# Attention probabilities of the selected and the window branch in one tile, with one run of keys, in a hybrid sparse-attention layer

## The chip, the cores and the metric

The kernel runs on one core of a Trainium2 chip. The metric is the device time of one execution in microseconds (us), median of several runs. Engines are named as the profile does: PE (TensorE), PEld (its weight loads), DVE (VectorE), ACT (ScalarE), POOL (GpSimd), SP (the queue that issues the DMAs).

## The reference, cut to what matters

One decoder layer on 512 rows of 1024 features. One projection of the normed input feeds two groups of eight heads of 64. The first group (NSA) attends in three branches with the same queries; each has its own keys and values, and its output is scaled by a gate:

```python
o_cmp, p_cmp = compressed_branch(qn, kc_cmp, vc_cmp)      # 31 compressed blocks
o_sel = selected_branch(qn, ks_r, heads(vs, G), sel_idx)  # top 16 of 8 blocks: all causal keys
o_win = window_branch(qn, kw_r, heads(vw, G))             # window 512 on 512 rows: all causal keys
o_nsa = g[..., 0:1] * o_cmp + g[..., 1:2] * o_sel + g[..., 2:3] * o_win
```

With these sizes the selected and the window branch are both plain causal attention over up to 512 keys. The second group (DSA) attends to the 128 keys with the highest indexer score:

```python
score = einsum('bths,bth->bts', relu(qi @ ki), wi)         # the indexer, 4 heads
_, idx = lax.top_k(where(causal, score, NEG), 128)
```

Both outputs are multiplied by their own SiLU gates, go through one output projection and are added to the input.

## The kernel before, in words

Every float32 operand of a product is split in two parts (hi and lo, of type fp32r), and a product is the sum of two or three products of parts, so nearly everything on PE comes in pairs or threes.

**Stages.** (1) `x` arrives; the projection of the indexer's columns (`I`) and the row norms. (2) Projection chunks `C` (raw compressed keys, line 400), `B` (keys and values of selected and window, line 390), with the indexer between them (lines 591, 612, 690) and its top-128 on DVE (lines 701 and 702), which gives masks. (3) Chunks `Q1`, `Q2`, `D` (queries), the compression network (`hid`, line 777), and from the end of `Q2` on the attention, woven with `D`, four gate chunks `Z` and the output projection (line 1220).

**Attention.** The work is cut in units: `n` or `d` (the group), query tile `i` of 128 rows, key head `g`, and for `n` a branch `b` (1 selected, 2 window, 0 compressed). The tiles' names carry them: `P_n302` is n, i=3, g=0, window. A unit goes through four blocks of 32 queries times 4 heads, which make 128 rows:

- Scores: `softmax_steps` multiplies a block's queries with the keys in `kn` (line 1011, two products hi and lo). Block `b` of tile `i` sees `128 i + 32 b + 32` keys. For i > 0 selected and compressed keys lie side by side and share a product, and the window's keys have their own; for i = 0 a copy of the window's first tile (two DMAs, `K_WIN0`) puts all three side by side, and each block multiplies all 288 columns.
- `softmax_of`: mask, scale and row minimum on DVE (line 983), a memset of the tile's ragged end (line 987), the exponential with its row sum on ACT (line 988), the reciprocal on DVE, and normalisation times the gate on POOL (line 1001). The probabilities `P` go to one of three rotating buffers, one per unit.
- `transposed`: for each key tile of 128, four PE transposes (line 1030) of the four blocks fill one PSUM bank; ACT copies it to `pth` (line 1031), DVE puts the rest in `ptl` (line 1032). Both have three buffers (`TBUFS`).
- `times_values`: two products of 512 columns (line 1041) with the values of that key tile, hi and lo side by side as 128 columns, add to the PSUM bank `o`.

For query tile i a selected and a window unit have i + 1 key tiles each. The last is the rows' own tile, in which block 0 sees 32 keys, block 1 64, block 2 96, block 3 128.

```python
us.v = [pair(vsw[:, j, g]) for j in range(i + 1)]
uw.v = [pair(vsw[:, j, 2 + g]) for j in range(i + 1)]
uw.S = lambda: softmax_steps(q, lambda b: [(k[:, :, 0:keys(b)], [win_(b)])])
```

**The order.** `attention` interleaves scores of later units with transposes and products of the present one, and `weave` fills other work in. Then `set_order` plans again: from a table of costs and due times it writes out a fixed order for every engine and for the DMA queue (`ROUNDS` passes; `URGENT`, `SOON`: when an engine waits for a more urgent instruction; `HURRY`: nanoseconds by which a named output is due earlier, empty here). An engine then executes its list strictly in order.

**Other lines that are spoken of.** `values_of` (lines 856 and 857) evacuates values, `kstack` and `key_parts` (lines 579 to 582, 591, 593) write transposed keys, `rope` (lines 532 to 538) rotates, `chunk_C` turns raw keys into compression inputs `FS` (lines 754 to 766), line 548 transposes the row norms.

Of the kernel before, what the change touches and what calls it, by code (L numbers as in the profile page):

```python
# [9 lines left out]
F32 = mybir.dt.float32  # L10
# [52 lines left out]
ARENA = 3689  # L63
# [3 lines left out]
RTB = 4  # L67

COST = 1 / 2400
TBUFS, AHEAD, LAG = 3, 2, 2  # L70
# [16 lines left out]
URGENT, SOON = 3000, 400  # L87
# [16 lines left out]
HURRY = {}  # L104
# [204 lines left out]
def tile_hybrid_layer(ctx, tc, xT, x, ng, win, gains, peT, w1, b1, w2, wout, cst, out):  # L309
# [128 lines left out]
    tri = carve([S + 384], BF16)  # L438
# [69 lines left out]
    trib = carve([S], BF16)  # L508
    nc.gpsimd.memset(trib, 0.0)
    nc.gpsimd.tensor_copy(trib[:, S - 32:], cs[:, C_TRIB:C_TRIB + 32])  # L510
# [6 lines left out]
    def tables(j, name):  # L517
        gn = gns[:, j, None, :]
        tab = work.tile([128, 2, NT, HD], F32, tag="tab", name="tab", bufs=3)
# [7 lines left out]

    def rope(dst, src_ps, nh, ct, st, p=128, add=None, tag="rt", wide=4):

        t2 = work.tile([128, wide, HD], F32, tag=tag + "2", name=tag + "2", bufs=RTB if tag == "rt" else 1)[:p, :nh, :]  # L530
# [53 lines left out]
    def kstack(dst, R, h0, nh):  # L584

        p = ps("T", "kT_ps")
        for t in range(NT):
            c = t * 128
            if nh == 1:

                nc.tensor.transpose(p[:, c:c + 128], R[:, t, h0:h0 + 2, :], ident)
            else:
                nc.tensor.transpose(p[:, c:c + 128], R[:, t, h0:h0 + nh, :], ident)
        if nh == 1:
            hi, lo = dst[0]
            nc.scalar.copy(hi, p)
            nc.vector.tensor_tensor(lo, p, hi.bitcast(F32), op=ALU.subtract)
            return
        for g in range(nh):
            key_parts(dst[g], p[g * HD:(g + 1) * HD, :], g)  # L600
# [252 lines left out]
    def values_of(p, t, dst):  # L853

        src_ = p.rearrange("p (c d) -> p c d", d=HD)
        nc.scalar.activation(dst[:, :, 0, :], src_, AF.Copy, scale=rstd[:, t:t + 1])
        nc.vector.scalar_tensor_tensor(dst[:, :, 1, :], src_, rstd[:, t:t + 1], dst[:, :, 0, :].bitcast(F32),
                                       op0=ALU.mult, op1=ALU.subtract)
# [17 lines left out]
    def b1_first():  # L876
        load_w1(0)
        ST["kb_raw"] = [work.tile([128, NT, 2, HD], F32, tag="m2", name=f"kb_raw{b}", bufs=2) for b in range(2)]
# [10 lines left out]

    def kb_stack():  # L890
        for b in range(2):
            kstack([two(k, slice(0, S) if b else slice(K_SEL, None)) for k in kn], ST["kb_raw"][b], 0, 2)
            if b:
                for k in kn:
                    nc.sync.dma_start(k[:, :, K_WIN0:K_CMP].bitcast(F32), k[:, :, 0:128].bitcast(F32))
            yield 0.4
# [72 lines left out]
    def softmax_of(u, b, src_, mask):  # L969

        n = src_.shape[-1]
        if b == 0:
            if u.b == 0 and u.kind == "n":
                u.P = pcs[:, turn_c[0] % (AHEAD + 1)]
                turn_c[0] += 1
            else:
                tag, bufs = ("P0", 4) if u.name[:2] == "n0" else ("P", AHEAD + 1)
                w = 128 * u.i + 128
                u.P = work.tile([128, 4, w], F32, tag=tag, name="P_" + u.name, bufs=bufs)
            u.m, u.l = mls[:, turn[0] % 8, 0], mls[:, turn[0] % 8, 1]  # L980
            turn[0] += 1
        P, m, l = u.P[:, b, :n], u.m, u.l
        nc.vector.tensor_tensor_reduce(P, src_, mask, u.r[:, b:b + 1], 3e38, op0=ALU.add, op1=ALU.min,  # L983
                                       accum_out=m[:, b:b + 1])
        if b == 0 and u.P.shape[-1] > 32:

            nc.vector.memset(u.P[:, 0:3, u.P.shape[-1] - 96:], 0.0)
        nc.scalar.activation(P, P, AF.Exp, bias=m[:, b:b + 1], scale=-1.0, accum_out=l[:, b:b + 1])  # L988
        if b == 3:
# [7 lines left out]
            else:  # L997

                for bb in range(4):
                    Pb = u.P[:, bb, :128 * u.i + 32 * bb + 32]  # L1000
# [15 lines left out]
    def transposed(u, j, parts):  # L1016
# [11 lines left out]
        else:  # L1028
            for h in range(4):
                nc.tensor.transpose(p[:, h * 128:(h + 1) * 128], u.P[:, h, j * 128:(j + 1) * 128], ident)  # L1030
            nc.scalar.copy(ph, p)  # L1031
            nc.vector.tensor_tensor(pl, p, ph.bitcast(F32), op=ALU.subtract)  # L1032
        parts.append((u, j, ph, pl))

    def times_values(u, j, *parts):
        if u.first and j == 0:
            u.o[0] = ps("O", "o" + u.name)
        o = u.o[0]
        end = u.last and j == len(u.v) - 1
        for x, pp in enumerate(parts):  # L1040
            nc.tensor.matmul(o, u.v[j], pp, start=(u.first and j == 0 and x == 0), stop=(end and x == 1))  # L1041
        if end:
            if u.dst is None:
                u.dst = work.tile([128, 2, 128], F32, tag="od", name="od_" + u.name, bufs=2)
# [5 lines left out]
    def pv_steps(u, parts):  # L1050

        for j in range(len(u.v) if u else LAG):
            if u:
                transposed(u, j, parts)
# [21 lines left out]
    def units_of(kind, i, g, done):  # L1076
        n = 128 * (i + 1)
        q, o = [None], [None]
        res = []
        order = (1, 2, 0) if kind == "n" else (0,)  # L1080
        for b in order:
# [3 lines left out]
            u.q, u.o, u.done = q, o, done  # L1085
# [12 lines left out]
        causal = lambda b: trib[:, S - keys(b):]  # L1098
        if kind == "d":
            u.v = [pair(vd[:, j, g]) for j in range(i + 1)]  # L1100
            if g == 0 and i:

                mm = work.tile([128, 4, n], BF16, tag="mm", name=f"mm{i}", bufs=2)
# [7 lines left out]
        us, uw, uc = res  # L1111
        us.v = [pair(vsw[:, j, g]) for j in range(i + 1)]
        uw.v = [pair(vsw[:, j, 2 + g]) for j in range(i + 1)]
        uc.v = [pair(vcs[:, g])]
        k = kn[g]
        sel = lambda b, c: (us, slice(c, c + keys(b)), causal(b))
        win_ = lambda b: (uw, slice(0, keys(b)), causal(b))
        cmp = lambda b, c: (uc, slice(c, c + 32), cmask[:, 30 - 8 * i - 2 * b:62 - 8 * i - 2 * b])

        if i == 0:  # L1120
            us.S = lambda: softmax_steps(q, lambda b: [
                (k[:, :, K_WIN0:K_SEL + 128], [sel(b, 160), win_(b), cmp(b, 128)])])
        else:
            uw.S = lambda: softmax_steps(q, lambda b: [(k[:, :, 0:keys(b)], [win_(b)])])
            us.S = lambda: softmax_steps(q, lambda b: [
                (k[:, :, K_CMP:K_SEL + keys(b)], [sel(b, 32), cmp(b, 0)])] if keys(b) + 32 <= 512 else [
                (k[:, :, K_SEL:], [sel(b, 0)]), (k[:, :, K_CMP:K_SEL], [cmp(b, 0)])])
# [33 lines left out]
    def attention(units):  # L1161
# [8 lines left out]
        for k in range(-AHEAD, len(units) + 1):  # L1170
# [5 lines left out]
            yield from interleave(pv, itertools.chain(*s), 2 * len(u.v) if u else 1, 5)  # L1176
# [17 lines left out]
    def mix(half, i, g):  # L1194

        o = on[i, g] if half == 0 else od[f"{i}{g}"]
        m = b8.tile([128, 2, 2, 128], F32R, tag=f"mx{half}{g}", name="mx", bufs=2)
# [84 lines left out]
    weave(att, "n000", [  # L1282
# [17 lines left out]
    for i in (2, 1, 0):  # L1300
        weave(att, f"n{i}10", [out_half(i + 1, 0)], RA, X3)
# [98 lines left out]
```

## Time and profile before

| | |
|---|---|
| median of 3 runs | 312.7 us (312.56 to 312.94) |
| the profiled execution's own time | 312.76 us |
| its span, first to last instruction | 311.0 us, granted TensorE clock 1.000 |
| PE, PEld busy | 306.0, 258.9 us |
| DVE, ACT, POOL busy | 263.0, 241.0, 234.6 us |
| DMA | 32.16 MB, 103 GB/s |

The profiled execution is 0.06 us above the median and 1.8 us longer than its span. A matmul's duration in a row is that of one instruction from entry to its modelled end, and matmuls overlap; what one costs PE is the distance from its start to the next one's start, which the timeline shows.

### The profile page before, as it was taken

Reading aid. Unit: us, or ns where it says so; the run is one execution under the profiler, and the core shown is the slowest. Engines: PE = TensorE matmul, PEld = TensorE weight load, DVE = VectorE, ACT = ScalarE, POOL = GpSimd, SP = SyncE. Lnnn points to the kernel's source line nnn. Section 1 sums busy time; section 2 is a strip of 40 time slices with the busy share of each in tenths; the row PEclk is TensorE's granted clock in tenths of the full one; section 3 lists DMA queues with packets and bytes.
Section 4 is the critical chain, followed back from the end, with each engine's and each line's share of the span. In section 5 each row is a group of like instructions: output and inputs, shape, how many; then the busy total and the mean of one; then the engine's idle time right before and its main releaser. Section 6 shows DMA issues by size and latency. Waiting matters only on the chain.

```text
span 311.0 us, 6033 instructions
## 1 busy us (share of the span) xinstructions
PE 306.0 (98%) x1681; PEld 258.9 (83%) x1681; DVE 263.0 (85%) x797; ACT 241.0 (78%) x794; POOL 234.6 (75%) x416
## 2 busy tenths in 40 slices
PE   8999999999999999999999999999999999999995
PEld 4997788999888878888888888888888888888885
DVE  4998635699999999999999999999999999886501
ACT  6964656879997999898999989874379997985500
POOL 2099897997997599894789978995779895767500
PEclk9999999999999999999999999999999999999999
DMA  7994353552421033400031042233445252012011
GB/s 283 414 366 119 100 179 107 163 178 70 119 54 34 2 86 94 144 2 3 16 89 36 5 136 74 72 106 87 134 109 163 70 166 81 4 45 90 8 62 67
DMA packets 21249, 32.16 MB, mean 103 GB/s; under 512 B 5664, under 2 KB 8480, under 8 KB 21216
## 3 DMA queue, kind: packets, MB, share of 16 engines
q1 hardware_dynamic: 21216, 31.78, 32.6%
q8 instruction: 13, 0.21, 0.3%
q14 instruction: 20, 0.16, 0.2%
HBM read 29.04 MB, written 2.47 MB: 101 GB/s over the span
## 4 chain that ended last, share of the span: by engine, by line
PE 88%; DVE 7%; issue 1%; ACT 1%; DMA 1%; DVEq 0%; ACTq 0%
PE out L1220 15%; PE z L400 14%; PE Q L390 11%; PE on L1041 7%; PE D L390 7%; PE B L390 6%; PE s_n L1011 6%; PE T_n L1030 6%; PE od L1041 3%; PE T_d L1030 3%; PE s_d L1011 3%; PE hid L777 2%; DVE xsq L471 1%; PE idx L690 1%; PE qT_ps L612 1%
## 5 line engine op out<-in xcount | busy, mean ns | idle before, releaser
L988 ACT ACTIVATE P_n<-P_n,arena 128x416 f32<-128x416 f32 (+9 forms) x64 | 33.5, 524 | 5.7 <-DVE arena L983 3.5
L983 DVE CUSTOM_DVE_ANT_0 P_n<-s_n,arena 128x416 f32<-128x416 f32 (+9 forms) x64 | 30.7, 492 | 2.0 <-PE s_n L1011 1.2
L1001 POOL TENSOR_SCALAR P_n<-P_n,arena 128x416 f32<-128x416 f32 (+7 forms) x64 | 30.4, 493 | 1.5
L1011 PE MATMUL s_n<-kn,arena_r 128*128 128x288 f32 (+12 forms) x116 | 28.6, 326 | 0.0
L1032 DVE TENSOR_TENSOR ptl<-T_n,pth 128x512 fp32r<-128x512 f32 x40 | 27.0, 677 | 0.5 <-ACT pth L1031 0.4
L701 DVE MAX8 m<-scores 128x8 f32<-128x512 f32 (+2 forms) x48 | 26.6, 554 | 0.7
L400 PE MATMUL z<-hThi,whi_Z 128*128 128x512 f32 x64 | 26.4, 413 | 0.0
L702 DVE MATCH_REPLACE8 scores<-m,scores 128x512 f32<-128x512 f32 (+2 forms) x48 | 26.0, 542 | 0.1
L1030 PE MATMUL T_n<-arena,P_n 128*128 128x128 f32 x160 | 26.0, 272 | 0.0
L400 PE MATMUL z<-hTlo,whi_Z 128*128 128x512 f32 x64 | 25.5, 398 | 0.0
L400 PE MATMUL z<-hThi,wlo_Z 128*128 128x512 f32 x64 | 25.3, 398 | 0.0
L1031 ACT CAST pth<-T_n 128x512 fp32r<-128x512 f32 x40 | 23.2, 584 | 1.5 <-PE T_n L1030 1.2
L1011 PEld LDWEIGHTS s_n<-kn,arena_r 128*128 128x128 f32 x116 | 20.9, 188 | 4.0
L1030 PEld LDWEIGHTS T_n<-arena,P_n 128*128 128x128 f32 x160 | 20.2, 140 | 4.9 <-POOL P_n L1001 0.2
L1220 PE MATMUL out<-whi_wo,mx 128*128 128x512 f32 (+1 forms) x72 | 24.2, 384 | 0.0
L1220 PE MATMUL out<-wohi,mx 128*128 128x512 f32 (+1 forms) x72 | 23.9, 375 | 0.0
L357 POOL TENSOR_TENSOR wlo_Z<-raw_Z,whi_Z 128x512 fp32r<-128x512 f32 x16 | 20.5, 1294 | 3.5 <-ACT whi_Z L356 3.5
L390 PE MATMUL Q<-wlo_Q,hThi 128*128 128x256 f32 (+1 forms) x64 | 22.0, 343 | 0.0
L390 PE MATMUL Q<-whi_Q,hTlo 128*128 128x256 f32 (+1 forms) x64 | 21.8, 341 | 0.0
L390 PE MATMUL Q<-whi_Q,hThi 128*128 128x256 f32 (+1 forms) x64 | 21.8, 341 | 0.0
L357 POOL TENSOR_TENSOR w1l<-raw_w,w1h 128x512 fp32r<-128x512 f32 x16 | 20.6, 1300 | 0.0
L988 ACT ACTIVATE P_d<-P_d,arena 128x416 f32<-128x416 f32 (+15 forms) x32 | 16.7, 521 | 5.0 <-DVE arena L983 4.9
(264 smaller groups left out, 1101.5 us busy)
## 6 DMA issues: line engine op xcount, KB each, us to landing
raw_w<-in_w_dram SPq DMA_DIRECT2D x16, 256.0 KB, 3.6
raw_Z<-in_win_dram SPq DMA_DIRECT2D x16, 256.0 KB, 2.7
wor<-in_wout_dram SPq DMA_DIRECT2D x16, 256.0 KB, 2.8
raw_Q<-in_win_dram SPq DMA_DIRECT2D x12, 256.0 KB, 2.9
raw_D<-in_win_dram SPq DMA_DIRECT2D x8, 256.0 KB, 2.9
xres<-in_x_dram SPq DMA_DIRECT2D x8, 256.0 KB, 2.9
out_dram<-xres SPq DMA_DIRECT2D x7, 256.0 KB, 2.0
xw<-in_xT_dram SPq DMA_DIRECT2D x2, 860.0 KB, 7.9
```

What stands on the lines that cost most here:

```text
L357: engine.tensor_tensor(lo, raw, hi.bitcast(F32), op=ALU.subtract)
L390: nc.tensor.matmul(out_ps, a[:, k, tsl], b, start=(k == 0 and b is hi and a is hT["hi"]), stop=(k == KB - 1 and a is hT["lo"]))
L400: nc.tensor.matmul(out_ps, b[:, csl], a[:, k, :], start=(k == 0 and b is hi and a is hT["hi"]), stop=(k == KB - 1 and b is lo))
L701: nc.vector.max(m8, sc)
L983: nc.vector.tensor_tensor_reduce(P, src_, mask, u.r[:, b:b + 1], 3e38, op0=ALU.add, op1=ALU.min, accum_out=m[:, b:b + 1])
L988: nc.scalar.activation(P, P, AF.Exp, bias=m[:, b:b + 1], scale=-1.0, accum_out=l[:, b:b + 1])
L1001: nc.gpsimd.tensor_scalar(Pb, Pb, l[:, bb:bb + 1], 1.0 if u.gate is not None else 0.5, op0=ALU.mult, op1=ALU.mult)
L1011: nc.tensor.matmul(p, q[0][:, b], k[:, x], start=(x == 0), stop=(x == 1))
L1030: nc.tensor.transpose(p[:, h * 128:(h + 1) * 128], u.P[:, h, j * 128:(j + 1) * 128], ident)
L1032: nc.vector.tensor_tensor(pl, p, ph.bitcast(F32), op=ALU.subtract)
L1041: nc.tensor.matmul(o, u.v[j], pp, start=(u.first and j == 0 and x == 0), stop=(end and x == 1))
L1220: nc.tensor.matmul(p, a, b[:, csl], start=(k == 0 and b is hi and a is mx[0]), stop=(k == 7 and a is mx[1]))
```

## The change

For i and g the probabilities of the selected and the window branch lie in one tile of `256 i + 256` columns. Blocks 0 and 1 keep only the first 64 keys of the own tile, and these 64 of selected and 64 of window lie side by side, so that one transpose and one product serve both branches; the values for it (`vm`: selected's first 64 rows above, window's first 64 below) are gathered by two DMAs of 256 KB. Blocks 2 and 3 still have an own tile for each branch. To make the window's part start with the own tile, its keys are stored from the last tile to the first with the halves of a tile exchanged, and its values with exchanged halves. Window keys, compressed keys and selected keys then are one run in `kn`, so that for i < 2 one score product per block serves all three while they fit 512 columns; the two DMAs to `K_WIN0` go. The window branch scores 64 or 128 keys of the own tile instead of 32, 64, 96, 128. The own tile's products have 256 columns.

Besides: `TBUFS` 3 to 2, `URGENT` 3000 to 2000, `SOON` 400 to 300, `HURRY` 4000 for the indexer's score banks, the units of i = 0 run compressed first, and `P`, `od`, tables and rope temporaries have a name each in place of rotating buffers.

```diff
-TBUFS, AHEAD, LAG = 3, 2, 2
+TBUFS, AHEAD, LAG = 2, 2, 2
-URGENT, SOON = 3000, 400
+URGENT, SOON = 2000, 300
-HURRY = {}
+HURRY = {'idx': 4000}
...
-    trib = carve([S], BF16)
+    trib = carve([2 * S + 32], BF16)
...
 def values_of(p, t, dst, parts=((slice(0, 128), slice(0, 128)),)):
+        for a, b in parts:
+            nc.scalar.activation(dst[b, :, 0, :], src_[a], AF.Copy, scale=rstd[a, t:t + 1])
...
-        values_of(p[:, 256:], t, vsw[:, t])
+        values_of(p[:, 256:384], t, vsw[:, t, 0:2])
+        a, b = slice(0, 64), slice(64, 128)
+        values_of(p[:, 384:], t, vsw[:, t, 2:4], ((a, b), (b, a)))
...
+        for x in range(2):
+            h = slice(64 * x, 64 * x + 64)
+            nc.sync.dma_start(ST["vm"][h].bitcast(F32), v[h, :, 2 * x:2 * x + 2])
...
-        if b == 0 and u.P.shape[-1] > 32:
+        if b == 0 and u.kind == "d":
             nc.vector.memset(u.P[:, 0:3, u.P.shape[-1] - 96:], 0.0)
+        if b == 0 and u.kind == "n" and u.b == 1:
+            nc.vector.memset(u.P[:, 0:3:2, 128 * u.i + 96:128 * u.i + 128], 0.0)
...
+            for b, c in blocks:
+                nc.tensor.transpose(p[:, b * 128:(b + 1) * 128], u.P[:, b, c:c + 128], ident)
+            cols = slice(128 * blocks[0][0], 512)
+            nc.scalar.copy(ph[:, cols], p[:, cols])
+            nc.vector.tensor_tensor(pl[:, cols], p[:, cols], ph[:, cols].bitcast(F32), op=ALU.subtract)
...
+        half = lambda b: 64 if b < 2 else 128
+        us.c0 = lambda b: 128 - half(b)
+        uw.c0 = lambda b: 128 * i + 128
+        uw.keys = lambda b: 128 * i + half(b)
+        us.items = [tile_of(us, 128 * j, v(j, 0)) for j in range(i)]
+        uw.items = [([(b, uw.c0(b) + half(b) + 128 * (i - 1 - j)) for b in range(4)], [(whole, v(j, 1))]) for j in range(i)]
+        lo_, hi_ = slice(0, 256), slice(256, 512)
+        uw.items.append(([(b, 128 * i + (64 if b < 2 else 0)) for b in range(4)], [(lo_, ST["vm"][:, i, g]), (hi_, v(i, 0))]))
+        uw.items.append(([(b, 128 * i + 128) for b in (2, 3)], [(hi_, v(i, 1))]))
...
+        if i < 2:
+            res[0].S = lambda: softmax_steps(q, lambda b: [
+                (k[:, :, S - nw(b):K_SEL + ns(b)], [sel(b, nw(b) + 32), win_(b), cmp(b, nw(b))])]
+                if nw(b) + 32 + ns(b) <= 512 else rest_(b) + [(k[:, :, at_w(b)], [win_(b)])])
```

How the order of the instructions moves, at the two places that the prediction speaks of.

PE, the own tile of query tile 1, g = 0 (`T_n`: a bank of transposes, `on`: the output bank, `pth` and `ptl`: the transposed probabilities, `arena_r`: values). Before, the transposes of the own tile of the selected and then of the window branch, and further on their products:

```order
L1030 MATMUL T_n_2267<-arena,P_n_2055 128x128 x4
...
L1030 MATMUL T_n_2340<-arena,P_n_2190 128x128 x4
...
L1041 MATMUL on_2322<-pth,arena_r 128x512
...
L1041 MATMUL on_2322<-ptl,arena_r 128x512
```

Now, the shared tile, the rest of the window's own tile, and their products:

```order
L1054 MATMUL T_n_2321<-arena,P_n_2055 128x128 x4
...
L1054 MATMUL T_n_2364<-arena,P_n_2055 128x128 x2
...
L1068 MATMUL on_2358<-pth,vm 128x256
L1068 MATMUL on_2358<-ptl,vm 128x256
L1068 MATMUL on_2358<-pth,arena_r 128x256
L1068 MATMUL on_2358<-ptl,arena_r 128x256
```

Eight transposes have become six, and four products of 512 columns (a `pth` and a `ptl` for either branch) have become six of 256: the four shown, and a pair with `arena_r` for the window's blocks 2 and 3.

PE, from the transposes of the row norms (`rrow_ps`) to the indexer's key transposes (`kT_ps`) and query transposes (`qT_ps`), with chunk `C` around them. Before:

```order
L548 MATMUL rrow_ps<-arena 128x128 x4
...
L400 MATMUL C_451<-hThi,wlo_C_323 128x512
L591 MATMUL kT_ps<-arena,ridx 128x128 x2
L400 MATMUL C_451<-hThi,whi_C_330 128x512
...
L612 MATMUL qT_ps<-arena,ridx 128x128 x2
```

Now:

```order
L555 MATMUL rrow_ps<-arena 128x128 x4
...
L621 MATMUL qT_ps<-arena,ridx 128x128
...
L401 MATMUL C_453<-hTlo,whi_C_324 128x512
L598 MATMUL kT_ps<-arena,ridx 128x128 x4
L401 MATMUL C_453<-hThi,wlo_C_325 128x512
...
L699 MATMUL idx_570<-kix,arena_r 128x512
```

Between `rrow_ps` and the first key transpose stand 28 products of 512 columns before (3 of `C`, 13 of `B`, 12 of `C`) and 21 now (3, 10 and 8), with two query transposes among them. All four key transposes now stand together, and the indexer's first score product (`idx`) follows five products of `C` later; before, it came behind all of chunk `B`.

## Rows read from the trace of the kernel before

**Rows 1.** The page, busy time of each engine, and the clock by 40 slices

```profile
PE 306.0 (98%) x1681; PEld 258.9 (83%) x1681; DVE 263.0 (85%) x797; ACT 241.0 (78%) x794; POOL 234.6 (75%) x416
PEclk9999999999999999999999999999999999999999
```

**Rows 2.** Stretches: us, busy PE, PEld, DVE, ACT, POOL (instructions), clock, DMA share, GB/s

```profile
20.00:45.00 25.00, 24.64 (x113) 19.63 (x113) 17.56 (x61) 11.73 (x39) 23.66 (x26) 1.00 0.53 166
45.00:70.00 25.00, 25.00 (x153) 22.04 (x152) 17.86 (x43) 19.36 (x66) 22.30 (x36) 1.00 0.50 150
95.00:156.00 61.00, 61.00 (x332) 51.07 (x331) 58.45 (x211) 56.84 (x239) 48.45 (x106) 1.00 0.17 47
200.00:260.00 60.00, 60.00 (x325) 50.91 (x325) 57.46 (x175) 46.38 (x128) 48.99 (x65) 1.00 0.38 111
```

**Rows 3.** All waits of PE: us in total, times, longest us

```profile
PE I L443 <- DVE arena L445: 1.4, 1, 1.4
PE kT_ps L591 <- DVE FS L766: 0.4, 1, 0.4
```

**Rows 4.** Timeline of PE in the attention: start us, us, instruction

```profile
200.74 0.46 PE L1011 MATMUL s_n<-kn,arena_r 128*128 128x320 f32 x2
201.04 0.60 PE L1030 MATMUL T_d<-arena,P_d 128*128 128x128 f32 x4
201.39 0.48 PE L400 MATMUL z<-hThi,whi_Z 128*128 128x512 f32 x1
201.71 0.39 PE L400 MATMUL z<-hTlo,whi_Z 128*128 128x512 f32 x1
...
202.18 0.39 PE L1041 MATMUL od<-pth,arena_r 128*128 128x512 f32 x1
202.41 0.40 PE L1041 MATMUL od<-ptl,arena_r 128*128 128x512 f32 x1
202.64 0.39 PE L400 MATMUL z<-hThi,whi_Z 128*128 128x512 f32 x1
```

**Rows 5.** Timeline of PE at the end, products of 256 columns, nine from start to start

```profile
306.01 0.40 PE L1220 MATMUL out<-wohi,mx 128*128 128x256 f32 x2
...
307.07 0.40 PE L1220 MATMUL out<-wohi,mx 128*128 128x256 f32 x2
```

**Rows 6.** Groups of PE and PEld by line: count, busy us, mean ns

```profile
L1030 PE MATMUL T_n<-arena,P_n 128*128 128x128 f32 x160 | 26.0, 272 | 0.0
L1041 PEld LDWEIGHTS on<-ptl,arena_r 128*128 128x128 f32 x48 | 9.1, 189 | 1.0
```

**Rows 7.** Timeline of PE and DVE before the indexer

```profile
25.09 0.15 DVE L434 COPY arena<-vx_ps 128x4 f32<-128x4 f32 x1
...
25.29 0.65 PE L548 MATMUL rrow_ps<-arena 128*128 128x128 f32 x4
...
27.45 0.42 DVE L532 TENSOR_TENSOR rt<-I,arena 128x256 f32<-128x256 f32 x1 [0.30 <-ACT rest L631]
...
31.98 1.26 DVE L766 TENSOR_TENSOR FS<-ff,FS 128x496 fp32r<-128x496 f32 x2
32.05 0.39 PE L400 MATMUL C<-hThi,wlo_C 128*128 128x512 f32 x1
...
32.80 0.41 PE L591 MATMUL kT_ps<-arena,ridx 128*128 128x128 f32 x2 [0.36 <-DVE FS L766]
```

**Rows 8.** Groups of DVE and ACT by line: count, busy us, mean ns

```profile
L987 DVE MEMSET P_n<- 128x288 f32 x16 | 4.8, 298 | 0.2
L1032 DVE TENSOR_TENSOR ptl<-T_n,pth 128x512 fp32r<-128x512 f32 x40 | 27.0, 677 | 0.5 <-ACT pth L1031 0.4
L857 DVE SCALAR_TENSOR_TENSOR arena_r<-Q,arena,arena_r 128x128 fp32r<-128x128 f32 x4 | 1.4, 351 | 0.4 <-ACT arena_r L856 0.3
L1031 ACT CAST pth<-T_n 128x512 fp32r<-128x512 f32 x40 | 23.2, 584 | 1.5 <-PE T_n L1030 1.2
```

**Rows 9.** The top-128 by its line: ns min/median/max, first and last start us

```profile
L701 DVE MAX8 m<-scores x48: 414/552/696, 62.8 to 229.9; 128x8 f32<-128x512 f32 x16, 128x8 f32<-128x384 f32 x16, 128x8 f32<-128x256 f32 x16
```

More of the change, by code (lines that the diff above doesn't have):

```diff
@@ L877, in b1_first @@
         load_w1(0)
-        ST["kb_raw"] = [work.tile([128, NT, 2, HD], F32, tag="m2", name=f"kb_raw{b}", bufs=2) for b in range(2)]
+        ST["kb_raw"] = [work.tile([128, NT, 2, HD], F32, tag=f"kb_raw{b}", name=f"kb_raw{b}", bufs=1) for b in range(2)]
         ST["ss_kb"] = sums("kb")
@@ L1014, in softmax_steps, with transposed @@
                 yield 2 * COST * max(n, 256)
-    def transposed(u, j, parts):
+    def transposed(u, item, parts):
         p = ps("T", "T_" + u.name)
@@ L1028, in transposed, with times_values @@
         else:
[L1029 to L1036, printed above, removed]
+            blocks = item[0]
+            for b, c in blocks:
[3 more added lines that the diff above has]
+            nc.vector.tensor_tensor(pl[:, cols], p[:, cols], ph[:, cols].bitcast(F32), op=ALU.subtract)
+        parts.append((u, item, ph, pl))
+    def times_values(u, item, *parts):
+        first = u.o[0] is None
+        if first:
             u.o[0] = ps("O", "o" + u.name)
         o = u.o[0]
-        end = u.last and j == len(u.v) - 1
-        for x, pp in enumerate(parts):
-            nc.tensor.matmul(o, u.v[j], pp, start=(u.first and j == 0 and x == 0), stop=(end and x == 1))
+        end = u.last and item is u.items[-1]
+        for cols, v in item[1]:
+            for x, pp in enumerate(parts):
+                nc.tensor.matmul(o[:, cols], v, pp[:, cols], start=(first and x == 0), stop=(end and x == 1))
         if end:
             if u.dst is None:
-                u.dst = work.tile([128, 2, 128], F32, tag="od", name="od_" + u.name, bufs=2)
+                u.dst = work.tile([128, 2, 128], F32, tag="od_" + u.name, name="od_" + u.name, bufs=1)
                 od[u.name[1:3]] = u.dst
@@ L1050, in pv_steps @@
     def pv_steps(u, parts):
-        for j in range(len(u.v) if u else LAG):
+        for item in (u.items if u else [None] * LAG):
             if u:
-                transposed(u, j, parts)
+                transposed(u, item, parts)
                 yield 0.43
@@ L1084, in units_of @@
             u.name = f"{kind}{i}{g}{b}"
-            u.q, u.o, u.done = q, o, done
+            u.q, u.o, u.done, u.pair = q, o, done, pair_
+            u.c0 = lambda b: 0
+            u.keys = lambda b: 128 * i + 32 * b + 32
             u.dst = on[i, g] if kind == "n" else None
@@ L1097, in units_of @@
         keys = lambda b: 128 * i + 32 * b + 32
-        causal = lambda b: trib[:, S - keys(b):]
+        causal = lambda b: trib[:, S + 64 - keys(b):S + 64]
+        whole = slice(0, 512)
+        tile_of = lambda u, c, v: ([(b, u.c0(b) + c) for b in range(4)], [(whole, v)])
         if kind == "d":
-            u.v = [pair(vd[:, j, g]) for j in range(i + 1)]
+            u.items = [tile_of(u, 128 * j, pair(vd[:, j, g])) for j in range(i + 1)]
             if g == 0 and i:
-                mm = work.tile([128, 4, n], BF16, tag="mm", name=f"mm{i}", bufs=2)
+                mm = work.tile([128, 4, n], BF16, tag=f"mm{i}", name=f"mm{i}", bufs=1)
                 v = mbias[i].rearrange("(b r) n -> r b n", b=4)
@@ L1110, in units_of @@
             return res
[L1111 to L1114, printed above, removed]
+        us, uw, uc = (res[order.index(b)] for b in (1, 2, 0))
+        half = lambda b: 64 if b < 2 else 128
+        us.c0 = lambda b: 128 - half(b)
+        uw.c0 = lambda b: 128 * i + 128
+        uw.keys = lambda b: 128 * i + half(b)
+        v = lambda j, b: pair(vsw[:, j, 2 * b + g])
+        us.items = [tile_of(us, 128 * j, v(j, 0)) for j in range(i)]
@@ L1117, in units_of @@
-        win_ = lambda b: (uw, slice(0, keys(b)), causal(b))
+        nw, ns = uw.keys, us.keys
+        own = lambda b: trib[:, 0:nw(b)] if b % 2 else trib[:, S + 32:S + 32 + nw(b)]
+        sel = lambda b, c: (us, slice(c, c + ns(b)), causal(b))
+        win_ = lambda b: (uw, slice(0, nw(b)), own(b))
         cmp = lambda b, c: (uc, slice(c, c + 32), cmask[:, 30 - 8 * i - 2 * b:62 - 8 * i - 2 * b])
-        if i == 0:
-            us.S = lambda: softmax_steps(q, lambda b: [
-                (k[:, :, K_WIN0:K_SEL + 128], [sel(b, 160), win_(b), cmp(b, 128)])])
-        else:
[L1124 to L1127, printed above, removed]
+        at_w = lambda b: slice(S - nw(b), S)
@@ L1175, in attention @@
             pv = pv_steps(u, parts) if k >= 0 else ()
-            yield from interleave(pv, itertools.chain(*s), 2 * len(u.v) if u else 1, 5)
+            yield from interleave(pv, itertools.chain(*s), 2 * len(u.items) if u else 1, 5)
     wo = {}
```

83 lines of the change are left out of this document (48 added, 35 removed).

## The prediction

> **What bounds the kernel.** I read first the page's busy times: PE 98% of the span, DVE 85%, ACT 78%, POOL 75%, the TensorE clock full in every slice [rows 1]. A busy PE need not be a PE at its limit, so I read next what PE waited for: in 311 us the profile names two waits, 1.4 us at the very start and 0.36 us before the indexer's key transposes [rows 3]. Then the timeline, for what an instruction costs PE from its start to the next one's: the two products of 512 columns at 202.18 and 202.41 take 0.23 us each, the one after them starts at 202.64 [rows 4]. So PE runs back to back from about 20 us to the end, and every microsecond of PE work that goes shortens the run, if the other engines keep up. Last, the stretches: from 95 to 156 us DVE is busy for 58.45 of 61 us and ACT for 56.84, from 200 to 260 us DVE for 57.46 of 60 [rows 2]. DVE is nearly a second bound there. Its free time lies early: 7.4 us from 20 to 45 and 7.1 us from 45 to 70 [rows 2], while the top-128 starts only at 62.8 us and ends at 230 [rows 9].
>
> **What PE sheds.** The counts are those of the code; there are 8 pairs of i and g.
>
> Transposes: per pair 4 (2i + 2) before and 4 (2i + 1) + 2 now, 2 less, 16 in all. A group of four followed by a product of 512 starts at 201.04, and the product after that at 201.71: 0.67 us less the product's 0.23 leaves 0.44, or 0.11 us a transpose [rows 4]. That is 1.76 us. (The 272 ns of the group's row [rows 6] is entry to end, with overlap.)
>
> Products with values: per pair four of 512 become six of 256. 32 x 0.23 = 7.36 us go. Nine products of 256 columns with changing weights take 306.01 to 307.07, 0.118 us each [rows 5], so 48 x 0.118 = 5.66 us come. Gain 1.7 us.
>
> Scores: 12 products fewer; the columns of all score products fall by 512, because the merged runs of i = 0 and 1 save more than the window's 64 extra columns per pair and pass cost. Two products of 320 take 0.30 us [rows 4], 0.47 ns a column, so 0.24 us; four products become so narrow (128 columns) that they cost a transpose's 0.11 rather than 0.06 us, which gives back 0.2. I take 0.1 us gain.
>
> Sum: 1.76 + 1.7 + 0.1 = **3.6 us** of PE work.
>
> The Trainium skill has a rule against this: its page "TensorE: Matmul & The Clock Gate", section "Back-to-back issue gap", says that in a stream with weight loads a product of 512 columns costs about 131 ns and one of 128 about 81, so that width costs little and count much. On a line through these two (an estimate) transposes give 1.3 us, scores 0.8, and the products with values lose 0.5, in all 1.6 us instead of 3.6. The trace does not agree: 0.23 us at 512 columns and 0.118 at 256, nearly in proportion.
>
> **What the other engines get.** DVE: of the 16 memsets (298 ns) eight go and eight shrink to 64 columns, at least 2.4 us gone [rows 8]; eight of the 40 subtractions into `ptl` halve, at half of 677 ns some 2.7 us; the evacuation of chunk `B`'s values adds 12 operations of 128 columns or fewer for 4 of 256, at 351 ns [rows 8] at most 4.2 us more, but these lie before 70 us, where DVE has room [rows 2]. The window's 64 extra columns per pair add 512 columns to each of mask, exponential and normalisation, at `ptl`'s 677 / 512 = 1.3 ns a column 0.7 us each. ACT: eight copies into `pth` halve, 8 x 584 / 2 = 2.3 us less [rows 8], against up to 4.2 us more before 70 us. So in the attention DVE sheds 2.4 + 2.7 - 0.7 = 4.4 us and ACT 2.3 - 0.7 = 1.6, while PE sheds 3.6, and the earlier indexer lets the top-128 use DVE's free 14.5 us before 70 us. I count no wait for them there, and none saved, since before shows none on PE [rows 3]. The cover is PE's own work; should it be gone, it is DVE at 58 of 61 us that shows next. POOL gets one more small cast and some memset before 20 us and 0.7 us of normalisation; it stands at 75% [rows 1]. On SP's queue the two `kn` copies go, and two `vm` transfers wait for the last values of `B`; behind them stand the last weight loads of the compression network and of `Q2`, which are not used before the next two chunks; cost nothing.
>
> **What the early indexer costs.** Before, the key transposes waited 0.36 us, because their bank came free with the first `FS` of line 766, which starts at 31.98 [rows 7]. Now PE comes to them after seven products fewer, 7 x 0.23 = 1.6 us, less 0.2 for the query transposes in between: 1.4 us earlier. The `FS` chain stands at the same place in DVE's list. If it ends when it did, PE waits 1.4 us longer. It may end sooner: the ropes no longer alternate with ACT's copies, which cost DVE 0.30 us twice, once at 27.45 [rows 7]. On the other side, the row norms' last copy (25.09 [rows 7]) now stands behind three more small rope operations, some 0.15 to 0.2 us each by its own row, and PE's `rrow_ps` behind it, at most 0.5 us. So the loss lies between nothing, or 0.4 us gained should the old wait vanish, and 1.4 + 0.5 = 1.9 us, with 0.4 on top for each of two query evacuations that may slip in ahead on DVE: 2.7. I take **0.6 us**, nearer to the lower end, since both gaps of 0.30 and the old wait's 0.36 come off the 1.9 and the chain has less around it.
>
> **Sum.** 312.76 (profiled) - 3.6 + 0.6 = 309.8; the median before is 0.06 lower, so **309.7 us**. Bounds: all of the early loss absent and the old wait gone, 312.7 - 3.6 - 0.4 = 308.7, with the row-to-row spread of the durations (0.1 us on each of the three terms) and some of DVE's lighter load showing, 308.1; the early loss at its worst, 312.7 - 3.6 + 2.7 = 311.8.
>
> **The rivals.**
>
> *Two buffers instead of three.* `pth` and `ptl` now have two. In the planned order the transposes of an item stand before the last product of the item two before it in 60 of 66 cases (with three buffers: 11 of 65), so ACT's copy must wait for PE, PE's next product for ACT's 584 ns and DVE's 677 [rows 8], and on ACT the exponentials queue behind the copy. That closes a loop of 0.58 + 0.68 + 0.23 = 1.5 us plus three hand-overs. For it: ACT is 93% busy from 95 to 156 us [rows 2], so a held copy hurts. Against it: an item's share of the attention's 190 us is 190 / 68 = 2.8 us. It decides once PE loses 3.0 us by it: 8 waits like the one of 0.36 [rows 3] make no change, 10 make it slower, 12 give 312.7 - 3.0 + 4.3 = 314.0 us. Chance 0.08.
>
> *Products do not shrink with their width.* If a product of 256 must sit out its own weight load, it costs 0.189 us [rows 6] and not 0.118: 48 x 0.189 = 9.1 us for 7.36, a loss of 1.7 where I have a gain, and 312.7 - 1.76 - 0.1 + 1.7 + 0.6 = 313.1 us. Against it: the nine of [rows 5] have such loads too. Chance 0.02. A milder form is a fixed share in each product: a line through a transpose's 0.11 us at 128 columns and 0.23 at 512 [rows 4] gives 0.15 at 256, so the products with values gain 7.36 - 7.2 = 0.16 instead of 1.7, the scores 12 x 0.07 + 512 x 0.31 ns = 1.0, and the run takes 312.7 - 1.76 - 0.16 - 1.0 + 0.6 = 310.4 us. Chance 0.05. The section of the Trainium skill's page "TensorE: Matmul & The Clock Gate" named above has this form with a flatter line; by its 1.6 us the run would take 311.7. [rows 5] speak against both.
>
> *The change doesn't do what it says.* PE's saved time is idle because DVE, at 58.45 of 61 us [rows 2], paces the attention after all: its work there falls by about 2.4 + 2.7 - 0.7, but the top-128, if not really earlier, stays. Then what goes of DVE's idle share (2.5 of 61) is all that can be gained, near 0.4 us with the early loss on top: 312.7 us. Chance 0.06.
>
> *DVE's relief shows.* Small unnamed stretches between products also close: under 308.1 us. Chance 0.04.
>
> **How the numbers follow.** The forecast with its early loss has 0.75 and spans 308.1 to 311.8, and the fixed share's 0.05 lies inside. What is outside is 0.08 + 0.02 + 0.06 + 0.04 = 0.20. A measurement here tells 0.2%, 0.6 us, from no change: faster is under 312.1. Faster: 0.75 + 0.05 + 0.04 + a part of the "not what it says" case, 0.02 = 0.86. Same: 0.04 of that case and 0.02 of the weight loads, 0.06. Slower: 0.08.
>
> **What the profile after would show.** Right: 144 transposes of `T_n` at line 1054 where line 1030 had 160, 48 products of 256 columns 0.118 us apart, PE still without named waits after 40 us, the first top-128 row well before 62.8 us, DVE's busy share in the attention below 95%, one or two waits of PE between 25 and 35 us of 0.3 to 1.5 us together. Wrong: PE waits at the products with `pth` (the two buffers), products of 256 columns 0.19 us apart, or PE waits at line 1054 for POOL or DVE.

## The result and the profile after

| | before | after |
|---|---|---|
| median | 312.63 us (312.27 to 312.94, 4 runs) | 308.24 us (308.08 to 308.48, 4 runs) |
| profiled execution, span | 312.76, 311.0 us | 308.21, 306.4 us |

The ratio is 0.986 (95% interval 0.9847 to 0.9872): 4.4 us faster, 1.5 us below the forecast of 309.7 us and just above the lower end of its range, 308.1.

The page and the stretches of the changed kernel, beside [rows 1] and [rows 2]. First the busy times:

```profile
PE 301.3 (98%) x1669; PEld 256.4 (84%) x1669; DVE 261.0 (85%) x797; ACT 240.7 (79%) x802; POOL 235.4 (77%) x418
```

Then the stretches (us, busy PE, PEld, DVE, ACT, POOL with instructions, clock, DMA share, GB/s):

```profile
20.00:45.00 25.00, 24.93 (x117) 19.93 (x116) 22.26 (x70) 14.68 (x40) 23.35 (x25) 1.00 0.53 171
45.00:70.00 25.00, 25.00 (x158) 22.68 (x157) 23.50 (x63) 20.51 (x79) 24.69 (x38) 1.00 0.57 156
...
95.00:156.00 61.00, 61.00 (x337) 51.44 (x335) 57.27 (x207) 58.18 (x246) 50.53 (x106) 1.00 0.21 56
...
200.00:260.00 60.00, 60.00 (x323) 50.72 (x321) 52.30 (x157) 45.52 (x125) 45.51 (x61) 1.00 0.37 112
```

PE is still the bound, 98% of a span that is 4.6 us shorter. DVE works earlier: 22.26 and 23.50 us in the first two stretches where [rows 2] have 17.56 and 17.86, and 52.30 instead of 57.46 late. The top-128 by its line (ns min/median/max, first and last start) begins 18 us earlier than in [rows 9]:

```profile
L710 DVE MAX8 m<-scores x48: 412/549/697, 44.6 to 219.2; 128x8 f32<-128x512 f32 x16, 128x8 f32<-128x384 f32 x16, 128x8 f32<-128x256 f32 x16
```

The own tile of one pair in the timeline of PE (start us, us, instruction), four of its six products:

```profile
181.05 0.29 PE L1068 MATMUL on<-pth,vm 128*128 128x256 f32 x1
181.17 0.28 PE L1068 MATMUL on<-ptl,vm 128*128 128x256 f32 x1
181.29 0.28 PE L1068 MATMUL on<-pth,arena_r 128*128 128x256 f32 x1
181.41 0.28 PE L1068 MATMUL on<-ptl,arena_r 128*128 128x256 f32 x1
181.52 0.40 PE L401 MATMUL z<-hThi,whi_Z 128*128 128x512 f32 x1
```

From 181.05 to 181.52 four products take 0.47 us, 0.118 each, as forecast. The groups by line (count, busy us, mean ns, idle before and what ended it), beside [rows 6] and [rows 8]:

```profile
L1054 PE MATMUL T_n<-arena,P_n 128*128 128x128 f32 x144 | 24.1, 273 | 0.0
L1057 DVE TENSOR_TENSOR ptl<-T_n,pth 128x512 fp32r<-128x512 f32 x32 | 21.8, 680 | 3.0 <-ACT pth L1056 2.6 <-POOL arena L1016 0.2
...
L1056 ACT CAST pth<-T_n 128x512 fp32r<-128x512 f32 x32 | 18.7, 583 | 2.5 <-PE od L1068 1.6 <-PE on L1068 0.6
...
L1057 DVE TENSOR_TENSOR ptl<-T_n,pth 128x256 fp32r<-128x256 f32 x8 | 3.3, 416 | 0.6 <-ACT pth L1056 0.4
...
L1056 ACT CAST pth<-T_n 128x256 fp32r<-128x256 f32 x8 | 2.9, 365 | 0.3 <-PE T_n L1054 0.2
```

The two buffers do show, but on ACT and DVE: the copy into `pth` now waits for a product that still reads its buffer (1.6 + 0.6 us for the banks `T_n`), which it did not in [rows 8]. No wait of PE for either has a row.

The early part, beside [rows 7]; first DVE, then PE:

```profile
25.30 0.15 DVE L435 COPY arena<-vx_ps 128x4 f32<-128x4 f32 x1
25.38 0.74 DVE L539 TENSOR_TENSOR rt<-I,arena 128x256 f32<-128x256 f32 x2
...
27.36 1.83 DVE L764 TENSOR_TENSOR kt<-C,arena 64x256 f32<-64x256 f32 x4
...
30.55 0.67 DVE L776 TENSOR_TENSOR FS<-ff,FS 128x496 fp32r<-128x496 f32 x1
```

```profile
25.51 0.65 PE L555 MATMUL rrow_ps<-arena 128*128 128x128 f32 x4
...
31.10 0.60 PE L598 MATMUL kT_ps<-arena,ridx 128*128 128x128 f32 x4
```

`FS` starts 1.43 us earlier than before (31.98), the ropes stand in pairs and both gaps of 0.30 us are gone, and the key transposes at 31.10 have no wait behind their row. They start before the first `FS` has ended (30.55 + 0.67 = 31.22), so they no longer wait for it. All waits of PE now:

```profile
PE I L444 <- DVE arena L446: 1.2, 1, 1.2
PE Q L391 <- DVE kn L587: 0.6, 1, 0.6
```

The 0.36 us at `kT_ps` of [rows 3] are gone, and a new wait has come. Its place, PE and then DVE:

```profile
91.04 0.28 PE L787 MATMUL hid<-w1h,FS 128*128 128x256 f32 x1
91.95 0.47 PE L391 MATMUL Q<-whi_Q,hThi 128*128 128x512 f32 x1 [0.62 <-DVE kn L587]
```

```profile
88.38 0.54 DVE L711 MATCH_REPLACE8 scores<-m,scores 128x384 f32<-128x384 f32 x1
89.67 0.29 DVE L539 TENSOR_TENSOR rt<-Q,tab 128x128 f32<-128x128 f32 x1 [0.74 <-DMA dr_q<-nz]
...
91.45 0.35 DVE L868 SCALAR_TENSOR_TENSOR arena_r<-Q,arena,arena_r 128x128 fp32r<-128x128 f32 x1
```

From 91.04 to 91.95 are 0.91 us where a product of 256 columns leaves 0.12: 0.8 us lost. DVE stood still for 0.74 us before 89.67, for a DMA, and the last of its rows that reads `Q`, at 91.45, ends at 91.80, just ahead of PE's start. The row names `kn`, which follows at 91.71 on DVE. In the program the product waits for the semaphore value that the evacuation at 91.45 sets, and it writes the PSUM bank that this evacuation empties.

One more difference is in no named row: from the start of a product of 512 columns to the start of the next one are 232.4 ns on average before (626 such pairs after 20 us, those over 300 ns left out) and 230.2 ns after (606), in chunk `B` 233.2 and 227.4. What these 2.2 ns are is the subject of the last experiments.

### The profile page after: what moved, and what is told of

Same layout as the page of the kernel before. It is cut to its first block, busy times and chain, and to the rows that moved or that the text cites. A ratio compares the mean times of both kernels' runs of the same rounds, so it can differ in the third digit from the quotient of the medians.

```text
span 306.4 us, 5994 instructions
## 1 busy us (share of the span) xinstructions
PE 301.3 (98%) x1669; PEld 256.4 (84%) x1669; DVE 261.0 (85%) x797; ACT 240.7 (79%) x802; POOL 235.4 (77%) x418
## 4 chain that ended last, share of the span: by engine, by line
PE 86%; DVE 4%; ACT 4%; POOL 3%; DMA 2%; issue 1%; DVEq 0%; POOLq 0%
PE out L1268 15%; PE z L401 14%; PE Q L391 8%; PE D L391 7%; PE B L391 7%; PE on L1068 7%; PE s_n L1033 6%; PE T_n L1054 5%; PE od L1068 3%; PE T_d L1054 3%; PE s_d L1033 3%; PE C L401 2%; PE hid L787 2%; ACT hThi L467 2%; POOL wlo_Q L358 2%; PE idx L699 1%
## 5 line engine op out<-in xcount | busy, mean ns | idle before, releaser
L1010 ACT ACTIVATE P_n<-P_n,arena 128x416 f32<-128x416 f32 (+15 forms) x64 | 33.7, 528 | 4.7 <-DVE arena L1003 4.1
L1003 DVE CUSTOM_DVE_ANT_0 P_n<-s_n,arena 128x416 f32<-128x416 f32 (+15 forms) x64 | 31.0, 499 | 1.0 <-PE s_n L1033 0.4
L1023 POOL TENSOR_SCALAR P_n<-P_n,arena 128x416 f32<-128x416 f32 (+15 forms) x64 | 30.8, 501 | 1.2
L1057 DVE TENSOR_TENSOR ptl<-T_n,pth 128x512 fp32r<-128x512 f32 (+1 forms) x40 | 25.0, 627 | 3.6 <-ACT pth L1056 2.9
L1033 PE MATMUL s_n<-kn,arena_r 128*128 128x512 f32 (+11 forms) x104 | 27.1, 342 | 0.0
L1054 PE MATMUL T_n<-arena,P_n 128*128 128x128 f32 x144 | 24.1, 273 | 0.0
L1056 ACT CAST pth<-T_n 128x512 fp32r<-128x512 f32 (+1 forms) x40 | 21.5, 540 | 2.7 <-PE od L1068 1.6
L1054 PEld LDWEIGHTS T_n<-arena,P_n 128*128 128x128 f32 x144 | 18.1, 140 | 4.0
L1033 PEld LDWEIGHTS s_n<-kn,arena_r 128*128 128x128 f32 x104 | 18.1, 189 | 3.3 <-issue 0.2
L1068 PE MATMUL on<-pth,arena_r 128*128 128x512 f32 (+1 forms) x48 | 18.3, 382 | 0.0
```

What stands on the lines that cost most here:

```text
L1023: nc.gpsimd.tensor_scalar(Pb, Pb, l[:, bb:bb + 1], 1.0 if u.gate is not None else 0.5, op0=ALU.mult, op1=ALU.mult)
L1033: nc.tensor.matmul(p, q[0][:, b], k[:, x], start=(x == 0), stop=(x == 1))
L1054: nc.tensor.transpose(p[:, b * 128:(b + 1) * 128], u.P[:, b, c:c + 128], ident)
L1068: nc.tensor.matmul(o[:, cols], v, pp[:, cols], start=(first and x == 0), stop=(end and x == 1))
```

## Experiments

**What the shared tile is worth.** Theory: PE runs back to back and the price is the width, so each piece costs what the prediction took. Rivals: a fixed share in every product, or relief of DVE and ACT that does the work. In all three kernels the order of every engine is that of the changed kernel: an added PE instruction is set right behind its neighbour after the planning.

*More transposes.*

```diff
             for b, c in blocks:
                 nc.tensor.transpose(p[:, b * 128:(b + 1) * 128], u.P[:, b, c:c + 128], ident)
+            if len(blocks) == 2:
+                for x, (b, c) in enumerate(blocks):
+                    nc.tensor.transpose(p[:, x * 128:(x + 1) * 128], u.P[:, b, c:c + 128], ident)
```

> The changed kernel, with 16 more transposes: where the window's rest of the own tile is transposed (blocks 2 and 3), the same two blocks are transposed a second time into the unused half of the bank. Every other instruction and the order of all engines stay. If PE runs back to back and a transpose costs it 0.11 us, the time is 308.2 + 16 x 0.11 = 310.0 us. If the transposes saved lay beside other engines' work (PE paced by DVE and ACT), 0 to 0.9 us more: 308.2 to 309.1.

Measured: 309.99 us, ratio 0.9911 (0.9894 to 0.9928), so 1.6 to 1.75 us over the changed kernel for 16 transposes, 0.10 to 0.11 us each. The transposes that the change saves were on the path.

*Halves.*

```diff
-                nc.tensor.matmul(o[:, cols], v, pp[:, cols], start=..., stop=...)
+                whole = not first and cols == slice(0, 512)
+                for h in ((slice(0, 256), slice(256, 512)) if whole else (cols,)):
+                    nc.tensor.matmul(o[:, h], v, pp[:, h], start=..., stop=...)
```

> The changed kernel, in the same order, with 72 of the value products of 512 columns (all but the first of each output bank) cut in two of 256 columns: 144 for 72. If a product costs by its width (0.231 us at 512, 0.118 to 0.120 at 256), 72 x (0.236 to 0.240 - 0.231) = 0.4 to 0.65 us more: 308.6 to 308.9. If a product has a fixed share (0.15 us at 256), 72 x 0.069 = 5.0 us more: 313.2. If it must sit out its own weight load (0.189), 72 x 0.147 = 10.6 us more: 318.8.

Measured: 309.07 us, ratio 0.9887 (0.987 to 0.9905), 0.83 us more, with about 0.7 us of uncertainty either way from the two intervals. The groups show the cut products (of each 64, 16 had 256 columns before):

```profile
L1085 PE MATMUL on<-pth,arena_r 128*128 128x256 f32 x64 | 15.1, 297 | 0.0
L1085 PE MATMUL on<-ptl,arena_r 128*128 128x256 f32 x64 | 14.9, 293 | 0.0
```

In the timeline two halves take 0.23 us, from 112.52 to 112.75:

```profile
112.52 0.40 PE L1085 MATMUL on<-ptl,arena_r 128*128 128x256 f32 x2
112.75 0.41 PE L1085 MATMUL on<-pth,arena_r 128*128 128x256 f32 x2
```

0.83 / 72 = 12 ns for each cut by the times, so that a product of 256 columns would cost (231 + 12) / 2 = 121 ns; with the uncertainty that does not differ from the 118 taken, and in this trace value products of 256 columns that follow each other lie 118 ns apart (91 pairs under 160 ns). The fixed share (5.0 us) and the weight load (10.6 us) fall; every half had a weight load of its own. The section "Back-to-back issue gap" of the Trainium skill's page "TensorE: Matmul & The Clock Gate" does not hold for this kernel either: on a line through its two figures (an estimate) 256 columns cost 98 ns and 512 cost 131, and 72 cuts would have cost 4.7 us.

*The own tile whole again.*

```diff
-        uw.items.append(([(b, 128 * i + 128) for b in (2, 3)], [(hi_, v(i, 1))]))
+        uw.items.append(([(b, 128 * i + 128) for b in (2, 3)], [(whole, v(i, 1))]))
```

with the two added transposes of the first experiment and copies of 512 columns into `pth` and `ptl`.

> The changed kernel, in the same order, with the work that the shared tile saves put back: the window's rest of the own tile gets four transposes instead of two, copies into pth and ptl of 512 columns instead of 256 and two products of 512 columns instead of 256, eight times (the extra half adds to the output what does not belong there: blocks 0 and 1 get a second sum). By PE's work alone 16 x 0.11 + 16 x (0.231 - 0.119) = 1.76 + 1.79 = 3.55 us more: 311.8 us. ACT gets 2.3 us and DVE 2.7 us more work; if their relief is what the change gained beyond PE's 3.6 us, the time goes back to 312.4 or more. If PE's shed work did not count in full, below 311.

Measured: 311.55 us, ratio 0.9963 (0.9949 to 0.9977), 3.2 to 3.3 us over the changed kernel. The work is back on all three engines:

```profile
L1080 DVE TENSOR_TENSOR ptl<-T_n,pth 128x512 fp32r<-128x512 f32 x40 | 27.2, 682 | 4.3 <-ACT pth L1077 3.6 <-POOL arena L1033 0.2
...
L1077 ACT CAST pth<-T_n 128x512 fp32r<-128x512 f32 x40 | 23.2, 583 | 3.0 <-PE od L1093 1.6 <-PE on L1093 0.8 <-PE T_n L1075 0.4
```

The time is PE's work alone: the 2.1 us more on DVE (27.2 against 21.8 + 3.3) and the 1.6 us more on ACT (23.2 against 18.7 + 2.9) cost nothing beside it. But the kernel stays 1.2 us below the one before with nearly the same work on PE, so the change has gained by something else too.

**What the early indexer and its constants are worth.** Theory: the earlier top-128 gives the rest. Rivals: it costs something; or only the accident of each plan counts.

```diff
-HURRY = {'idx': 4000}
+HURRY = {'idx': 1000}
```

> The changed kernel with HURRY 1000 instead of 4000 for the indexer, planned anew: PE comes to the indexer's first key transpose after 217 instructions of its list instead of 164, as late as the kernel before came to its last one. If the early indexer neither costs nor gives anything, 308.2 us within what a new plan changes, which I put at 0.5. If its early top-128 is what gave the 0.8 us beyond the forecast of 3.6, 309.0. If the forecast's loss of 0.6 us is there but hidden by a gain elsewhere, 307.6.

```diff
-URGENT, SOON = 2000, 300
+URGENT, SOON = 3000, 400
-HURRY = {'idx': 4000}
+HURRY = {}
```

> The changed kernel with the planner's constants of the kernel before (HURRY empty, URGENT 3000, SOON 400), so the shared tile and the names of buffers without the early indexer: PE comes to the first key transpose after 218 instructions instead of 164. If hurry_1000 was 0.9 us faster only because its plan lacks the one wait of PE at 91 us (0.8 us in the changed kernel), 307.3 to 307.7 us, and the profile shows no wait above 0.3 us after 40 us. If the early indexer is worth something by itself, above 308.2. If the lower spacing of the products came from the constants, 309 or more.

```diff
-URGENT, SOON = 2000, 300
+URGENT, SOON = 3000, 400
```

> The changed kernel with URGENT 3000 and SOON 400 as before, HURRY 4000 kept; planned anew, key transposes after 178 instructions of PE. If the wait at 91 us is an accident of one plan, it is gone here and the time is 307.2 to 307.8 us. If an early indexer brings it about by pushing DVE's work around 90 us together, it is here again: 308.0 to 308.6.

```diff
-SPARE = 250
+SPARE = 245
```

> The changed kernel with SPARE 245 instead of 250, the planner's slack in ns for what PE reads: a constant that should mean nothing, but it gives a new plan (about a tenth of PE's rows stand elsewhere). If a new plan by itself moves the time by as much as hurry_1000, old_urgent and old_constants differ from the changed kernel, it lies anywhere from 306.5 to 309.9 and off 308.2 by 0.5 or more, with its own waits of PE. If plans of the same constants agree, 308.2 within 0.3.

| kernel | us | ratio to before (95%) | first top-128 at |
|---|---|---|---|
| changed | 308.24 | 0.986 (0.9847 to 0.9872) | 44.6 us |
| old_urgent | 306.55 | 0.9811 (0.9796 to 0.9826) | 47.5 us |
| spare_245 | 306.89 | 0.9818 (0.9802 to 0.9834) | 50.4 us |
| hurry_1000 | 307.34 | 0.9834 (0.9817 to 0.9851) | 62.1 us |
| old_constants | 309.92 | 0.9924 (0.9907 to 0.9941) | 64.2 us |

A constant that should mean nothing (SPARE) gains 1.3 us. The time does not follow the place of the top-128. It goes with the waits of PE in these five, here all of them in old_constants and then in old_urgent:

```profile
PE I L444 <- DVE arena L446: 1.2, 1, 1.2
PE qT_ps L621 <- POOL naf L577: 0.6, 1, 0.6
PE Q L391 <- ACT kn L586: 0.3, 1, 0.3
PE T_n L1054 <- DVE ptl L1057: 0.2, 1, 0.2
PE T_n L1054 <- POOL P_n L1023: 0.2, 1, 0.2
```

```profile
PE I L444 <- DVE arena L446: 1.2, 1, 1.2
```

spare_245 has the same single row as old_urgent, and both lie 1.3 to 1.7 us below the changed kernel, whose wait at 91 us is 0.8 of it; the rest is in no named wait, and old_urgent came out 0.65 us below the 307.2 that was expected at least. So that wait is an accident of one plan, as old_urgent's first theory had it, and hurry_1000 is no proof that the early indexer costs time: its wait at `Q` is down to 0.2 us. The first theory for old_constants was wrong: removing the early indexer did not give 307.5 but 309.9, with 1.3 us of named waits elsewhere. Whether its late top-128 brings these about, or again the plan, is not separated. old_urgent, faster than both kernels, is the best version found: 306.55 us.

**Two buffers in the kernel before.**

```diff
-TBUFS, AHEAD, LAG = 3, 2, 2
+TBUFS, AHEAD, LAG = 2, 2, 2
```

> The kernel before with two buffers for pth and ptl instead of three (TBUFS 2), planned anew. If two buffers cost PE nothing because the planner puts the copies early enough, as the changed kernel's trace suggests (only ACT and DVE wait in the ring), 312.7 us within 0.5. If they cost what the rival said, 12 waits of 0.36 us: 317, and PE waits for pth or ptl by name.

Measured: 313.81 us, ratio 1.0037 (1.0025 to 1.0049), 1.2 us slower, between the two expectations. PE names no wait for `pth` or `ptl`, only 0.3 us at scores (`s_n`, for DVE's mask) and 0.2 at `idx`. The rival's mechanism is not there; since this too is a new plan, what the 1.2 us are is left open. Three buffers in the changed kernel were not tried.

**Where the 2.2 ns a product come from.**

> The kernel before, unchanged, profiled once more. In its first profile a product of 512 columns followed by another takes 233 ns in the middle of chunk B, in the changed kernel 227. If that belongs to the program, it is 233 again and the time 312.7 us. If it belongs to the chip or the moment, it is 227 here too, and the time about 1 to 1.5 us lower than 312.7.

Measured: 312.7 us, and the same 232.4 ns over 626 pairs. The difference belongs to the program. The two programs differ in where tiles lie in SBUF: the compiled program's allocation puts the hi and lo parts of the projections' weights 64 bytes beyond a multiple of 128 in the kernel before, and at multiples of 128 in the changed one. Other operands (`kn`, `pth`, `ptl`, `kix`) move with them. (The order is the same in the next three kernels as in the one each is made from.)

```diff
-ARENA = 3689
+ARENA = 3689 + 16
```

> The kernel before with 16 unused words more in its first constant tile (ARENA 3705 for 3689): every instruction and the order of all engines are the same, but all that lies behind it in SBUF moves up by 64 bytes, so the weights' parts of the projections start at multiples of 128 bytes, as in the changed kernel, and no longer 64 beyond one. If the 233 ns of a product of 512 columns in chunk B come from that, they become 227, and with some 380 products 5.5 ns shorter and 220 by 1.6 the time falls by 2.1 to 2.4 us, to 310.3. If the address does not matter, 312.6 us and 233 ns again.

Measured: 310.84 us, ratio 0.9941 (0.9928 to 0.9954): 1.7 to 1.8 us faster with 64 unused bytes. In the middle of chunk `B` 48 products of 512 columns lie between the same two rows of PE's timeline, in the kernel before and in the shifted one:

```profile
44.77 0.39 PE L390 MATMUL B<-whi_B,hThi 128*128 128x512 f32 x1
...
55.98 1.09 PE L690 MATMUL idx<-kix,arena_r 128*128 128x512 f32 x4
```

```profile
43.72 0.39 PE L390 MATMUL B<-whi_B,hThi 128*128 128x512 f32 x1
...
54.64 1.07 PE L690 MATMUL idx<-kix,arena_r 128*128 128x512 f32 x4
```

11.21 / 48 = 233.5 ns before, 10.92 / 48 = 227.5 shifted. Over all pairs it is 232.4 and 229.7 ns: 626 x 2.7 = 1.7 us, nearly the whole gain. Not only chunk `B` gains: the products with values `on`, which read no projection weights, go from 233.1 to 230.7 ns, and the gate chunks from 230.1 to 228.5. The wait at `kT_ps` is gone as well (0.36 us), which the next kernel separates.

```diff
-ARENA = 3689
+ARENA = 3689 + 8
```

> The kernel before with 8 unused words in its first constant tile instead of 16: the same instructions and order, all behind it 32 bytes up, the weights' parts 96 bytes beyond a multiple of 128. If only a multiple of 128 bytes is fast and every other start costs the same, 312.6 us and 233 ns in chunk B. If a multiple of 64 is better than one of 32, above 313. If the gain of before_shifted was not the address of the operands but the wait of PE at the indexer's key transposes that is gone there, the rows of chunk B stay at 233 ns, that wait is gone here too, and the time is near 312.2.

Measured: 313.18 us, ratio 1.0023 (1.0012 to 1.0034), 0.7 us slower than before. Its two rows:

```profile
44.65 0.40 PE L390 MATMUL B<-whi_B,hThi 128*128 128x512 f32 x1
...
55.85 1.09 PE L690 MATMUL idx<-kix,arena_r 128*128 128x512 f32 x4
```

11.20 / 48 = 233.3 ns, and 233.3 over all pairs, 0.9 more than before: 626 x 0.9 = 0.6 us of the 0.7. The wait at `kT_ps` is gone here too and nothing is gained by it, so the place in SBUF made the difference.

> The changed kernel with the same 16 unused words more in its first constant tile, same instructions, same order: here the shift takes the weights' parts from multiples of 128 bytes to 64 beyond one, as in the kernel before. If the address matters, 227 ns become 233 and the time rises by 2.1 to 2.4 us, to 310.5. If not, 308.2 us within 0.3.

```diff
-ARENA = 3689 + 272 - 192
+ARENA = 3689 + 272 - 192 + 16
```

Measured: 308.96 us, ratio 0.9875 (0.9855 to 0.9895), against 0.986 unshifted: 0.5 to 0.7 us slower, where 2.1 to 2.4 were expected, and the intervals overlap. The rows say the same in small: 231.5 ns over all pairs instead of 230.2. Chunk `C` goes from 229.3 to 233.2 ns and the gate chunks from 229.2 to 232.4, but chunk `B` only from 227.4 to 229.1, and the chunks `Q` and the products `on` get 0.8 and 2.0 ns shorter. The direction agrees, the size does not, and a start 64 bytes beyond a multiple of 128 is not slow by itself; which operand's address counts, and how, stays open.

## Why the prediction was right, and where not

**The main term held.** PE's shed work was put at 3.6 us: 1.76 for transposes, 1.7 for products, 0.1 for scores. The runs give 1.6 to 1.75 for 16 transposes and 3.2 to 3.3 for both together, where 3.55 were expected. That PE gives back nearly every microsecond, that DVE and ACT need no term, and that a product shrinks with its width all held, the last against the rule of the Trainium skill that the prediction quotes. The scores' 0.1 us was not tested by itself, nor were the names of the buffers and the new order of i = 0.

**The step that failed is "What the early indexer costs", +0.6 us.** It took over from the kernel before that the key transposes' bank comes free with the first `FS`, and that the `FS` chain ends when it did. Neither held. In the changed program the transposes write another PSUM bank, and they wait for the semaphore value of the last operation of line 764, which reads `C`; its row ends at 29.19 (27.36 + 1.83), long before PE comes at 31.10. Besides, the chain started 1.4 us earlier: both gaps of 0.30 us are gone, and rope work of 64 columns now stands ahead of the row norms' copy. Even with the old bank PE would have waited about 0.3 us (an estimate: `FS` ends at 31.22, and PE followed it by 0.15 us in the kernel before). So the term was 0 and the old wait of 0.36 us went too: its lower bound, 0.4 us of gain.

**Two terms were missing.** The spacing of the products: the sum priced one of 512 columns at 0.23 us on both sides, yet 606 pairs at 230.2 instead of 232.4 ns are 1.3 us. No row before said that the change would move operands in SBUF. That their place is the cause is shown for the kernel before; in the changed kernel the shift brought back 0.5 to 0.7 us, so for the rest of the 1.3 it is argued. And "I count no wait for them there" was wrong once: 0.8 us at 91 us. Together: -3.3 (tile) - 0.4 (old wait) - 1.3 (spacing) + 0.8 (new wait) = -4.2 of the 4.4 us measured.

**What was luck.** That the time lies in the range is in part luck: the missing 1.3 and 0.8 us have opposite signs, and three other plans of the same kernel (306.55, 306.89 and 307.34 us) lie below its lower end of 308.1.

**The rivals.** Two buffers: in the ring of the changed kernel only ACT and DVE wait; the 1.2 us that two buffers cost in the kernel before have no wait of PE for them behind them. No shrinking and the fixed share: refuted by halves. DVE paces: refuted, own_tile_whole's extra 2.1 us on DVE cost nothing beyond PE's (the rival's own sum, 312.7 - 0.4 + 0.6, gives 312.9 and not 312.7). DVE's relief shows: the same run speaks against it, since DVE's work came back and the time rose by no more than PE's.

**The signs named for it.** 144 transposes, products 0.118 us apart, the early top-128 and DVE at 57.27 of 61 us (94%) came; PE without waits after 40 us did not, nor the wait between 25 and 35 us.

## What to carry to other kernels

Where PE runs back to back, price a change by distances from start to start, width by width: half-empty tiles laid side by side gave what those distances said. Before a difference of half a per cent is put down to a change, look whether the operands of the hot products still start where they did, and try a pad of 64 bytes. A planner's output moves by nearly as much for a constant without meaning (1.3 us here), so several plans of the same kernel belong in the comparison; here the two fastest were those in which PE waits for nothing after its start. And before a wait is carried over into a forecast, look whether the instruction still waits for the same thing: here the key transposes had come to another bank.

## What was not expected of the hardware

The time of a product depends on where its operands lie in SBUF. In the kernel before a product of fp32r parts with 512 columns takes 227.5 ns from start to start with the weights' parts at multiples of 128 bytes, 233.5 with them 64 bytes beyond and 233.3 with 96 (48 products of chunk `B`, same instructions and order; all that lies behind the first constant tile moved together). There 64 bytes of padding are worth 1.7 to 1.8 of 312.5 us. It is no rule of multiples of 128: in the changed kernel chunk `B` takes 229.1 ns with its weights 64 bytes beyond one, and that shift costs 0.5 to 0.7 us.
